# A two-layer decoder trunk: the last residual product of each layer as seven block products of sums

## The chip, the cores and the metric

The kernel runs on one core of one Trainium2 chip. The metric is the time of one launch in microseconds of device time. A measurement of this kernel is the median of a few runs.

## The reference

All data is fp32; 512 tokens, a width of 1024, two layers.

```python
# per layer
x = x + (g_conv*y_conv + g_attn*y_nsa + g_mla*y_mla) @ w_out      # "the mix"
x = x + memory_cross_attention(rmsnorm(x), rmsnorm(mem), ...)     # ends with @ w_xo
gate, up = split(rmsnorm(x, norm_ffn) @ w_gate_up, 2)             # 1024 -> 2 x 2816
x = x + (silu(gate) * up) @ w_down                                # 2816 -> 1024, "the down residual"
# after two layers
return rmsnorm(x, norm_final)
```

The change is about the last line of a layer, the product of the 512x2816 activation with `w_down`, added to `x`.

## The kernel before

**Products.** Every fp32 operand is split in two (`hilo`): a high part, cast by ACT (line 92), and the rest, subtracted by DVE (line 93). A product of two operands is three matmuls, high x high, high x low and low x high (lines 85 to 87 in `mm3`, 1143 to 1145 in `residual`). Weights come by a DMA on SP's queue into `raw` (`load`, two buffers of 1 MB) and are split there into `wh` and `wl` (`unit`, three buffers each, 128x1024).

**The down residual** (`residual`, line 1125). `row_units` loads two blocks of 128 rows of `w_down` at a time, all 1024 columns, 4 KB a row. For each of the 22 row blocks PE runs over four token tiles and two halves of columns; the eight sums fill all eight PSUM banks. The last two or three blocks are held back and run tile by tile, so that the tiles end one after another; after each, DVE adds the bank to `x` (line 1157) and `after(t)` stores the tile in layer 0, and normalises and stores it in layer 1. The activations were split in the FFN stage (`keep_act`), block by block, into slots that other tiles had left.

**Sums in DRAM.** The gate/up product is already made in seven block products. The sums of the blocks of `w_gate_up` that it needs lie in DRAM (`sums`) and are made by DMAs on POOL's queue, DRAM to DRAM, half of them plain copies and half accumulating: 128 DMAs of 320 KB a layer. They are paced: every product of three matmuls calls `tick`, and every fifth (from layer 0's down residual on every sixth) issues the next DMA, which waits for that matmul. In the stages of the FFN none is issued.

**Order.** A scheduler orders each engine's instructions ahead of time; an engine runs its queue strictly in that order. SP carries the loads of weights, POOL the paced DMAs, the stores of `x` between stages (`xd`) and the power of -1/2 of each norm (line 200, `rs`).

## Time and profile before

| | |
|---|---|
| median of 3 runs | 1941.39 us (1939.9 to 1941.57) |
| the profiled execution | 1943.2 us, of which the span 1941.5 us |
| PE, PE weight loads | 1913.9 us (99%), 1674.5 us (86%) |
| DVE, ACT, POOL | 71%, 50%, 12% |
| granted TensorE clock | 0.996 of full speed |
| DMA | 317.95 MB, mean 164 GB/s |
| chain that ended last | PE 80%, DVE 8%, issue 5%, DMA 4%, ACT 3% |

The span is from the first to the last instruction of the profiled execution. PE is the engine of the matmuls, PEld its weight loads, which overlap matmuls; DVE, ACT and POOL are the vector, scalar and GpSimd engines, SP issues DMAs. A layer's stages follow one another: the mix (to about 545 us in layer 0), cross attention, the FFN's gate/up (about 632 to 855), the down residual (855.1 to 975.9), then layer 1 with its down residual from 1812 to the end.

### The profile page before, as it was taken

How to read it: one execution, taken by the hardware profiler on the slowest of the kernel's cores; microseconds unless marked ns; L12 is line 12 of the kernel's file. 1: busy time of each engine (PE TensorE's matmuls, PEld its weight loads, DVE VectorE, ACT ScalarE, POOL GpSimd, SP SyncE). 2: the span in 40 equal slices, each digit the busy share in tenths (PEclk: the TensorE clock that was granted, in tenths of full speed). 3: DMA queues.
4: the chain of work that ended last, by engine and by line, in shares of the span. 5: the costliest groups of instructions: out<-in, count | busy, mean ns of one | idle time of the engine just before them, and what ended most of it. 6: DMA issues, size and time to landing. Idle time of an engine off the chain costs nothing.

```text
span 1941.5 us, 29100 instructions
## 1 busy us (share of the span) xinstructions
PE 1913.9 (99%) x11136; PEld 1674.5 (86%) x11136; DVE 1371.0 (71%) x2525; ACT 979.2 (50%) x1858; POOL 227.6 (12%) x380
## 2 busy tenths in 40 slices
PE   9999999999999999999999999999999999999998
PEld 8877888888887999998888878888888889999886
DVE  6989899764466877762279989986655677777523
ACT  5366557663355545541244755675634465545312
POOL 1211112112121000001211111111112010000000
PEclk9999999999999999999999999999999999999999
DMA  6676655567783455566666565445676525555531
GB/s 186 152 188 182 154 134 137 132 169 211 221 229 113 154 175 192 177 226 176 175 168 162 161 189 127 122 102 141 170 204 181 177 99 173 179 182 174 183 108 65
DMA packets 218871, 317.95 MB, mean 164 GB/s; under 512 B 14528, under 2 KB 172483, under 8 KB 218732
## 3 DMA queue, kind: packets, MB, share of 16 engines
q1 hardware_dynamic: 194028, 220.83, 34.8%
q0 software_dynamic: 21760, 88.10, 21.0%
q10 hardware_dynamic: 2944, 7.17, 1.1%
q8 instruction: 87, 1.43, 0.3%
q14 instruction: 52, 0.43, 0.1%
HBM read 307.64 MB, written 92.30 MB: 206 GB/s over the span
## 4 chain that ended last, share of the span: by engine, by line
PE 80%; DVE 8%; issue 5%; DMA 4%; ACT 3%; POOL 1%; SPq 0%; DVEq 0%; POOLq 0%; ACTq 0%
PE ps_mm L85 12%; PE ps_mm L87 12%; PE ps_mm L86 12%; PE ps_mm L1143 2%; PE ps_mm L1144 2%; PE ps_mm L1145 2%; PE ps_t L85 2%; PE ps_t L86 2%; PE ps_t L87 2%; PE ps_s L85 2%; PE ps_s L86 2%; PE ps_s L87 2%; DMA raw<-in_w_in_dram 2%; PE ps_t L960 2%; PE ps_t L1144 2%
## 5 line engine op out<-in xcount | busy, mean ns | idle before, releaser
L93 DVE TENSOR_TENSOR wl<-raw,wh 128x1024 fp32r<-128x1024 f32 (+5 forms) x382 | 451.2, 1185 | 377.2 <-ACT wh L92 375.7
L92 ACT CAST wh<-raw 128x1024 fp32r<-128x1024 f32 (+5 forms) x382 | 388.0, 1020 | 587.5 <-PE ps_pv L1145 198.7
L85 PE MATMUL ps_mm<-hTh,wh 128*128 128x512 f32 (+1 forms) x1152 | 415.4, 361 | 1.1 <-DVE kc L93 1.1
L87 PE MATMUL ps_mm<-hTh,wl 128*128 128x512 f32 (+1 forms) x1152 | 411.4, 358 | 0.8 <-DVE wl L93 0.8
L86 PE MATMUL ps_mm<-hTl,wh 128*128 128x512 f32 (+1 forms) x1152 | 412.0, 358 | 0.0
L87 PEld LDWEIGHTS ps_mm<-hTh,wl 128*128 128x128 f32 x1152 | 218.2, 190 | 33.4 <-DVE wl L93 1.9
L85 PEld LDWEIGHTS ps_mm<-hTh,wh 128*128 128x128 f32 x1152 | 218.5, 190 | 30.4 <-DVE kc L93 1.5
L86 PEld LDWEIGHTS ps_mm<-hTl,wh 128*128 128x128 f32 x1152 | 218.5, 190 | 26.5 <-issue 0.7
L356 POOL DMA_DIRECT2D sums<-in_w_gate_up_dram x192 | 119.6, 627 | 842.1 <-PE ps_mm L87 429.6
L463 DVE SCALAR_TENSOR_TENSOR ca<-u,vT,ca 128x512 f32<-128x512 f32 x240 | 177.1, 745 | 2.9
L923 ACT ACTIVATE P<-P,ss 128x512 f32<-128x512 f32 (+3 forms) x128 | 71.4, 558 | 55.9 <-DVE ss L920 55.0
L92 ACT CAST PTh<-ps_t 128x512 fp32r<-128x512 f32 (+4 forms) x136 | 70.4, 517 | 55.8 <-PE ps_t L960 45.0
L85 PE MATMUL ps_s<-rh,wh 128*128 128x256 f32 x320 | 90.6, 283 | 0.0
L86 PE MATMUL ps_s<-rl,wh 128*128 128x256 f32 x320 | 90.6, 283 | 0.0
L87 PE MATMUL ps_s<-rh,wl 128*128 128x256 f32 x320 | 90.6, 283 | 0.0
L356 POOL DMA_DIRECT2D sums<-sums x64 | 50.0, 782 | 275.4 <-PE ps_mm L87 130.1
L93 DVE TENSOR_TENSOR PTl<-ps_t,PTh 128x512 fp32r<-128x512 f32 (+2 forms) x120 | 71.3, 596 | 8.4 <-ACT PTh L92 7.5
L931 ACT ACTIVATE P<-P,sr 128x512 f32<-128x512 f32 (+3 forms) x128 | 63.1, 553 | 18.2 <-DVE sr L929 18.1
L85 PE MATMUL ps_mm<-op,wh 128*128 128x512 f32 (+1 forms) x192 | 68.7, 358 | 0.0
L86 PE MATMUL ps_mm<-op,wh 128*128 128x512 f32 (+1 forms) x192 | 68.2, 355 | 0.0
L87 PE MATMUL ps_mm<-op,wl 128*128 128x512 f32 (+1 forms) x192 | 68.1, 355 | 0.0
L200 POOL TENSOR_TENSOR rs<-rs,mhalf 128x1 f32<-128x1 f32 x32 | 23.1, 721 | 383.5 <-DVE rs L197 383.3
(553 smaller groups left out, 4574.1 us busy)
## 6 DMA issues: line engine op xcount, KB each, us to landing
sums<-in_w_gate_up_dram POOLq DMA_DIRECT2D x192, 320.0 KB, 4.4
raw<-sums SPq DMA_DIRECT2D x80, 512.0 KB
raw<-in_w_in_dram SPq DMA_DIRECT2D x32, 1024.0 KB
raw<-in_w_gate_up_dram SPq DMA_DIRECT2D x24, 1024.0 KB
raw<-in_w_down_dram SPq DMA_DIRECT2D x22, 1024.0 KB
sums<-sums POOLq DMA_DIRECT2D x64, 320.0 KB, 4.9
raw<-in_w_in_dram SPq DMA_DIRECT2D x26, 512.0 KB
raw<-in_w_gate_up_dram SPq DMA_DIRECT2D x20, 512.0 KB
```

What stands on the lines that cost most here:

```text
L85: nc.tensor.matmul(o, lh, rh, start=start, stop=False)
L86: nc.tensor.matmul(o, lh, rl, start=False, stop=False)
L87: tick(nc.tensor.matmul(o, ll, rh, start=False, stop=stop))
L92: nc.scalar.copy(hi, src)
L93: nc.vector.tensor_tensor(lo, src, f(hi), op=OP.subtract)
L356: d = nc.gpsimd.dma_start(dst, src, accum_op=op) if op else nc.gpsimd.dma_start(dst, src)
L463: nc.vector.scalar_tensor_tensor(c, u[:, j:j + T], cw[:, m, j:j + 1], c, op0=OP.mult, op1=OP.add)
L923: nc.scalar.activation(p[:, c], p[:, c], AF.Exp, bias=s[:, k:k + 1], scale=-1.0, accum_out=s[:, 4 + k:5 + k])
L931: nc.scalar.activation(P[k], P[k], AF.Copy, scale=r[:, k:k + 1])
L960: nc.tensor.transpose(tp[:, w:w + 128], P[k][:, j * 128:(j + 1) * 128], ident)
L1143: nc.tensor.matmul(o, xh, wh[:, r], start=k == 0, stop=False)
L1144: nc.tensor.matmul(o, xh, wl[:, r], start=False, stop=False)
```

## The change

The down residual becomes a 2x2 block product: the 22 row blocks of `w_down` are taken as even and odd ones, its columns as two halves, the tokens as two halves of 256. Seven products of sums take the place of eight. Four of the seven need sums of quarters of `w_down`: four more tensors in DRAM (`down`, 128-row blocks of 512 columns at a pitch of 528), made by the same paced DMAs, 88 a layer of 256 KB, after the 128 for gate/up. The activation's sides are made in the FFN stage by `keep_act` (two split, the others as plain sums) and, for products 2 to 6, split in the residual during the product before. The products run one behind the other, 11 row blocks by two token tiles each, in two PSUM banks at a time; the results are added to `x` (and to a partial sum `U`) behind each product. Weights come in quarters: per product three loads of 1, 1 and 0.75 MB with rows of 2 KB. The pace is every 4th product instead of the 5th, every 12th in the FFN stage (where before nothing was issued), and every 4th instead of the 6th from layer 0's down residual on.

```diff
+        W, V = w_gate_up[l], w_down[l]
+        up = [dr.tile([512, n], F32, name=f"up{l}_{i}") for i in range(4)]
+        down = [dr.tile([FFN // 2, 528], F32, name=f"down{l}_{i}")[:, 0:512] for i in range(4)]
+        def added(s, w):
+            for dst, src in ((s[0], w[1][0]), (s[2], w[0][0]), (s[1], w[0][0]), (s[3], w[0][1])):
+                yield dst, src, None
+            for dst, src in ((s[0], w[1][1]), (s[2], w[1][0]), (s[1], s[0]), (s[3], s[1])):
+                yield dst, src, OP.add
...
+            for j in range(FFN // 256):
+                yield from added([t[j * 128:(j + 1) * 128, :] for t in down],
+                                 [[V[(2 * j + e) * 128:(2 * j + e + 1) * 128, o:o + 512] for e in range(2)]
+                                  for o in (0, 512)])
...
+    def down_residual(W, sums, kept, xs, more_x, after):
...
+        def split(v):
+            h, lo = (new("op", (128, 2, 256), F32R, name=n)[:, 0:v.shape[1], :] for n in ("th", "tl"))
+            hilo(h, lo, v)
+            return h, lo
+        def fourth(n):
+            v = new("P", (128, 2, 256), name="t2")[:, 0:b11[n].shape[1], :]
+            nc.vector.scalar_tensor_tensor(v, b11[n], -1.0, b22[n], op0=OP.mult, op1=OP.subtract)
+            return split(v)
+        parts = [(quarters[0][:, :, low[0]], lambda n: None), (quarters[1][:, :, low[0]], fourth), (of[1], lambda n: split(b12[n])),
+                 (of[2], lambda n: split(b21[n])), (quarters[1][:, :, low[1]], lambda n: split(b11[n])),
+                 (of[0], lambda n: split(b22[n])), (of[3], lambda n: None)]
+        tags = (("t", "t"), ("s", "s"), ("mm", "mm"), ("mm", "pv"), ("t", "t"), ("s", "s"), ("mm", "mm"))
...
+        def done(i, t, p):
+            x, y = xs[t], xs[2 + t]
+            if i == 0:
+                U[t] = new("op", name="U")
+                nc.scalar.copy(U[t], p)
+                add(x[0], x[0], p)
+            elif i == 1:
+                add(x[0], x[0], p)
+            elif i == 2:
+                add(U[t], U[t], p)
+                later(y[0], U[t])
+            elif i == 3:
+                add(U[t], U[t], p)
+                later(x[1], U[t], OP.subtract)
+                later(y[1], U[t], OP.subtract)
+            elif i == 4:
+                add(x[1], x[1], p, OP.subtract)
+                after(t)
+            elif i == 5:
+                add(y[0], y[0], p)
+                add(y[1], y[1], p, OP.subtract)
+            else:
+                add(y[0], y[0], p)
+                after(2 + t)
...
+            for n in range(N):
+                j = 2 * n
+                if n % 2 == 0:
+                    m = min(4, nj - j)
+                    raw = load(lambda raw: [(raw.rearrange("p (k c) -> p k c", k=4)[:, 0:m], w[:, j:j + m, :])])
+                m = min(2, nj - j)
+                c = n % 2 * 1024
+                held.append((n, unit(raw[:, c:c + m * 512].rearrange("p (k c) -> p k c", k=m), (m, 512))))
+                then.append(ahead(n))
...
+    EVERY = 4
-    paced["every"] = 5
+    paced["every"] = EVERY
...
+        paced["every"] = 12
...
+        def keep_act(m, a, b, sign=1.0):
+            d = act_slot(m)
+            for i in range(2):
+                q = slice(i * 256, (i + 1) * 256)
+                nc.vector.scalar_tensor_tensor(d[i], a[:, q], sign, b[:, q], op0=OP.mult, op1=OP.mult)
+            hilo(d[2], d[3], d[0])
+            if m % 4 == 3 or m == FFN // 128 - 1:
+                (b11, b12), (b21, b22) = (h[0:2] for h in kept[-1])
+                tc.cur_priority += 100000
+                nc.vector.tensor_tensor(b11, b11, b12, op=OP.subtract)
+                nc.vector.tensor_tensor(b21, b22, b21, op=OP.subtract)
+                nc.vector.tensor_tensor(b21, b21, b11, op=OP.add)
+                nc.vector.tensor_tensor(b12, b22, b12, op=OP.subtract)
+                tc.cur_priority -= 100000
...
-            paced["every"] = 6
+            paced["issued"], paced["every"] = 0, EVERY
...
-        residual(lambda k: act[k], FFN // 128, w_down[l], xs, after, 3 if last else 2, {8: lambda: load_x(xd, xs)})
+        down_residual(w_down[l], down_sums, kept, xs, lambda: load_x(xd, xs), after)
```

DVE's queue in the down residual of layer 1, before: the end of the FFN stage, the 19 subtractions that are left (`wl`), and the first additions to `x`.

```order
L93 TENSOR_TENSOR a_18550<-k,a_18550 128x512
L93 TENSOR_TENSOR a_18568<-k,a_18568 128x512
L93 TENSOR_TENSOR wl<-raw,wh 128x1024 x19
L1157 TENSOR_TENSOR x<-x,ps_t 128x512 x2
L197 SCALAR_TENSOR_TENSOR rs<-ss 128x1
L213 SCALAR_TENSOR_TENSOR hn<-x,rs,gB 128x512 x2
```

And after, around the end of the fourth product (index 3); `tl` is the low part of an activation sum for the next product.

```order
L1212 TENSOR_TENSOR U<-U,ps_mm 128x512
L1212 TENSOR_TENSOR U<-U,ps_pv 128x512
L93 TENSOR_TENSOR wl<-raw,wh 128x1024 x2
L93 TENSOR_TENSOR tl<-a_18028,th 128x512
L93 TENSOR_TENSOR wl<-raw,wh 128x1024
L93 TENSOR_TENSOR tl<-a_19010,th 128x256
L1212 TENSOR_TENSOR x<-x,U 128x512
L93 TENSOR_TENSOR tl<-a,th 128x512
L1212 TENSOR_TENSOR x<-x,U 128x512
L93 TENSOR_TENSOR tl<-a,th 128x512
L93 TENSOR_TENSOR wl<-raw,wh 128x1024
```

Around the end of the sixth product (index 5) four additions stand in one row:

```order
L93 TENSOR_TENSOR wl<-raw,wh 128x1024
L93 TENSOR_TENSOR wl<-raw,wh 128x512
L93 TENSOR_TENSOR wl<-raw,wh 128x1024
L1212 TENSOR_TENSOR x<-x,ps_s 128x512 x4
L93 TENSOR_TENSOR wl<-raw,wh 128x1024 x4
```

Before, nothing stood between the weights' subtractions; now the splits of the activations and the additions stand between them.

POOL's queue around the cross-attention residual of layer 0, before: the last two sums, the stores of `x`, the four `rs` of the FFN's norm.

```order
L356 DMA sums_1_148<-sums_0_147 64x1280
L356 DMA sums_3_150<-sums_1_148 64x1280
L1298 DMA xd<-x 128x512 x3
L200 TENSOR_TENSOR rs<-rs,mhalf 128x1
L1298 DMA xd<-x 128x512
L200 TENSOR_TENSOR rs<-rs,mhalf 128x1
L1298 DMA xd<-x 128x512 x3
L200 TENSOR_TENSOR rs<-rs,mhalf 128x1
```

And after, with the new sums between them:

```order
L1416 DMA xd<-x 128x512 x2
L368 DMA down_0_151<-in_w_down_dram 128x512
L200 TENSOR_TENSOR rs<-rs,mhalf 128x1
L1416 DMA xd<-x 128x512 x2
L368 DMA down_2_153<-in_w_down_dram 128x512
L200 TENSOR_TENSOR rs<-rs,mhalf 128x1
L1416 DMA xd<-x 128x512
L368 DMA down_1_152<-down_0_151 128x512
L1416 DMA xd<-x 128x512 x2
L200 TENSOR_TENSOR rs<-rs,mhalf 128x1
```

The `rs` operations now stand behind DMAs that wait for a matmul, and one of them for the landing of another sum.

## Rows read from the trace of the kernel before

**Rows 1.** The page: span; busy us, share of the span and instructions of PE

```profile
span 1941.5 us, 29100 instructions
PE 1913.9 (99%) x11136; PEld 1674.5 (86%) x11136; DVE 1371.0 (71%) x2525; ACT 979.2 (50%) x1858; POOL 227.6 (12%) x380
```

**Rows 2.** Busy time by stage: down residuals of layers 0 and 1, FFN

```profile
core 0: us, PE busy (x) PEld busy (x) DVE busy (x) ACT busy (x) POOL busy (x), PEclk, DMA share, GB/s
855.10:975.90 120.80, 120.15 (x531) 99.08 (x530) 37.20 (x40) 28.20 (x36) 21.18 (x38) 1.00 0.67 187
1811.90:1931.80 119.90, 119.54 (x530) 98.50 (x530) 37.54 (x41) 28.67 (x38) 1.11 (x3) 1.00 0.28 100
640.00:860.00 220.00, 219.35 (x1812) 218.36 (x1811) 167.85 (x207) 111.67 (x163) 0.00 (x0) 1.00 0.56 181
```

**Rows 3.** Timeline of PE in layer 1's down residual: start, us, engine, line

```profile
1854.84 0.39 PE L1145 MATMUL ps_mm<-wh,al 128*128 128x512 f32 x1
1855.07 0.39 PE L1143 MATMUL ps_mm<-wh,ah 128*128 128x512 f32 x1
```

**Rows 4.** Waits of ACT and DVE, 858 to 966: us in total, times, longest

```profile
ACT wh L92 <- PE ps_pv L1145: 83.8, 20, 4.5
...
DVE wl L93 <- ACT wh L92: 76.5, 19, 4.3
```

**Rows 5.** Groups by line and shape, whole span: busy us, mean ns of one

```profile
L93 DVE TENSOR_TENSOR wl<-raw,wh 128x1024 fp32r<-128x1024 f32 x354 | 431.8, 1223 | 374.0 <-ACT wh L92 372.5
L92 ACT CAST wh<-raw 128x1024 fp32r<-128x1024 f32 x354 | 370.4, 1050 | 547.9 <-PE ps_pv L1145 194.3 <-PE ps_mm L86 99.8 <-DMA raw<-in_w_gate_up_dram 43.3
...
L1423 DVE TENSOR_TENSOR k<-ps_s,k 128x256 f32<-128x256 f32 x40 | 17.0, 424 | 1.4
L93 DVE TENSOR_TENSOR al<-k,ah 128x512 fp32r<-128x512 f32 x26 | 16.8, 684 | 0.0
...
L92 ACT CAST ah<-k 128x512 fp32r<-128x512 f32 x26 | 15.9, 620 | 0.1
...
L1157 DVE TENSOR_TENSOR x<-x,ps_mm 128x512 f32<-128x512 f32 x18 | 12.0, 678 | 0.0
```

**Rows 6.** DMA queues and issues, 855 to 960: packets, MB, share of 16 engines

```profile
q0 software_dynamic: 1925, 7.89, 36.3%
q1 hardware_dynamic: 4668, 11.30, 30.4%
...
sums<-in_w_gate_up_dram POOLq DMA_DIRECT2D x19, 320.0 KB, 4.2
sums<-sums POOLq DMA_DIRECT2D x6, 320.0 KB, 4.6
```

**Rows 7.** The same view, 884 to 888, where one accumulating DMA runs alone

```profile
q0 software_dynamic: 89, 0.37, 56.7%
```

**Rows 8.** Timeline around one gate/up load of 1 MB

```profile
785.50 0.37 SPq L101 DMA_DIRECT2D raw<-in_w_gate_up_dram  x1
...
790.64 1.05 ACT L92 CAST wh<-raw 128x1024 fp32r<-128x1024 f32 x1 [3.19 <-DMA raw<-in_w_gate_up_dram]
...
791.73 2.44 DVE L93 TENSOR_TENSOR wl<-raw,wh 128x1024 fp32r<-128x1024 f32 x2
...
794.61 0.28 PE L85 MATMUL ps_mm<-hTh,wh 128*128 128x256 f32 x1
```

**Rows 9.** Busy time of 20 us in layer 0's mix, columns as in rows 2

```profile
540.00:560.00 20.00, 20.00 (x134) 18.39 (x134) 11.20 (x18) 7.46 (x15) 5.12 (x7) 1.00 0.95 268
```

**Rows 10.** DMA issues in the FFN stage, 700 to 850

```profile
raw<-in_w_gate_up_dram SPq DMA_DIRECT2D x7, 1024.0 KB
```

**Rows 11.** Timeline of the end: the last matmul and the last addition

```profile
1933.40 0.39 PE L1145 MATMUL ps_pv<-wh,a 128*128 128x512 f32 x1
...
1934.30 0.68 DVE L1157 TENSOR_TENSOR x<-x,ps_pv 128x512 f32<-128x512 f32 x1
```

**Rows 12.** Timeline of POOL behind layer 0's cross-attention residual

```profile
628.26 0.54 POOL L1298 DMA_DIRECT2D xd<-x  x1 [2.09 <-DVE rs L197]
628.82 0.57 POOL L200 TENSOR_TENSOR rs<-rs,mhalf 128x1 f32<-128x1 f32 x1
```

More of the change, by code (lines that the diff above doesn't have):

```diff
@@ L355, in tick @@
             for dst, src, op in islice(paced["steps"], 1):
+                paced["issued"] += 1
                 d = nc.gpsimd.dma_start(dst, src, accum_op=op) if op else nc.gpsimd.dma_start(dst, src)
@@ L1173 @@
     xs = load_x(xin, [], (0,))
-    sums, paced["steps"] = summed(0)
-    paced["every"] = 5
+    sums, down_sums, paced["steps"] = summed(0)
+    paced["every"] = EVERY
     for l in range(L):
@@ L1302 @@
         last = l == L - 1
[L1303 removed]
+        assert paced["issued"] >= 128
+        paced["every"] = 12
         g_next = load_gain(norm_final if last else norm_mix[l + 1])
[L1305 to L1331 removed]
@@ new lines, with act_slot @@
+        kept = []
+        def act_slot(m):
+            if m % 4 == 0:
+                kinds = [(plain, F32)] * 2 + [(halved, F32R)] * 2
+                if m + 4 <= FFN // 128:
+                    group = [[home(*kind) for kind in kinds] for _ in range(2)]
+                else:
+                    group = [[t[:, i:i + 1, :] for t in (home(*kind) for kind in kinds[::2]) for i in range(2)]
+                             for _ in range(2)]
+                kept.append(group)
+            return [v[:, m % 4 // 2, :] for v in kept[-1][m % 2]]
@@ L1432 @@
                 nc.scalar.activation(g[j][:, q1], g[j][:, q1], AF.Silu)
-                nc.vector.scalar_tensor_tensor(g[j], g[j], -1.0, ka[j], op0=OP.mult, op1=OP.mult)
-                keep_act(m + j, g[j])
-        xs = []
+                keep_act(m + j, g[j], ka[j], -1.0)
+        assert not list(paced["steps"])
         if not last:
-            sums, paced["steps"] = summed(1)
-            paced["every"] = 6
-        if not last:
+            sums, next_down, paced["steps"] = summed(1)
+            paced["issued"], paced["every"] = 0, EVERY
             def after(t):
@@ L1448, in after @@
                     nc.sync.dma_start(out[0, t * 128:(t + 1) * 128, c * 512:(c + 1) * 512], h)
[L1449 removed]
+        xs = []
+        down_residual(w_down[l], down_sums, kept, xs, lambda: load_x(xd, xs), after)
+        if not last:
+            down_sums = next_down
         x_src = xd
```

109 lines of the change are left out of this document (66 added, 43 removed).

## The prediction

> **What bounds the kernel now.** I read first the page's busy shares [rows 1], then the busy time by stage [rows 2], the matmuls' rhythm [rows 3], what ACT and DVE wait for inside the stage that is changed [rows 4], the price list of the small operations [rows 5], and last the DMA queues of each stage [rows 6, 7, 9, 10], with two short pieces of the timeline at the places that the change makes thinner [rows 8, 12]. PE is busy 1913.9 us of a span of 1941.5, at a granted clock of 1.00 in every stage that I use, the upper of its two levels. In both down residuals PE is busy 120.15 of 120.80 us and 119.54 of 119.90 [rows 2]: there is no idle time to win there, only matmuls to leave out. ACT and DVE are at a quarter to a third of that stage, and both wait backwards, for PE: the cast into `wh` waited 83.8 us, 20 times, for a matmul to give a buffer back, and the subtraction into `wl` only follows the cast [rows 4]. So before, weights are early by 4 us per unit; that is the cover that the change spends.
>
> **Removed: 132 matmuls.** Before, a layer's residual has 22 x 4 x 2 x 3 = 528 products of 128x512; after, 7 x 11 x 2 x 3 = 462. Layer 0's stage lasts 120.80 us, so 0.2288 us each (the starts of two neighbours stand 0.23 apart [rows 3]; the 0.39 us of a record overlaps the next and is not the price). 66 x 0.2288 = 15.1 us a layer, **-30.2 us** for two. Nothing else lies beside these matmuls, so all of it is on the path as long as PE stays fed.
>
> **Tail.** Before, two additions of 0.68 us follow the last matmul, which starts at 1933.40, and the span ends 8.1 us later [rows 11]. After, the last product ends a token tile with one addition per half, tiles 0 and 1 long done: one addition less behind the end, about **-0.5 us**.
>
> **Added work on DVE and ACT in the residual.** A product of 66 matmuls takes 15.1 us. In that time DVE has five units of 1.223 and a half one of 0.68 (6.8 us), for most products the split of the activations for the next product (5.5 x 0.684 = 3.8), once a fourth sum (5.5 operations of the same size, 3.8), and 2 to 6 additions of 0.678 (1.4 to 4.1) [rows 5]. Seven products: 47.6 + 19.2 + 3.8 + 22 x 0.68 = 85.6 us of 105.7; the fullest, product 2 of 7, has 6.8 + 3.8 + 3.8 + 1.4 = 15.8 of 15.1. ACT has 5.5 x 1.05 + 5.5 x 0.62 = 9.2 of 15.1. So on the mean it fits, but DVE's spare time per unit falls from 4.0 us (76.5 in 19 [rows 4]) to (105.7 - 85.6) / 38.5 = 0.5. What is queued matters: behind product 6 of 7 four additions (2.7 us) stand in one row ahead of the next four `wl`; PE has 12 matmuls (2.7 us) per unit and up to three units in buffers. The lower bound is 0 (buffers cover it), the upper one 0.7 for the overfull product and 0.7 for each other of six boundaries: 5 us a layer. The trace has no such row; nearest are the waits of [rows 4], with 4 us of cover, so I take a little: 1.5 a layer, **+3**.
>
> **Added DMA traffic in layer 0's residual.** There the paced sums for the next layer run beside the weights. Before, the software queue took 36.3% of 105 us for 25 paced DMAs, 1.52 us of all engines each, and the hardware queue 30.4% for 11.30 MB, 2.82 us per MB [rows 6]. After, each weight byte range is read as seven half-width blocks: 7 x 2.75 MB (MiB) = 20.2 MB instead of 11.5, so 57 us; and 154 of the counted products fall here, every fourth issues one: 38 x 1.52 = 58 us. Sum 115 us for a stage of 105.7 us. That is over full, by 9 us if no paced DMA slips into the next stage, and less if some do (nothing waits for them there until much later). Against a large loss: the mix of before ran a slice of 20 us at a DMA share of 0.95 with PE busy 20.00 [rows 9]. Bounds 0 and 9; I take **+6**, nearer the upper, since the loads have only two buffers. In layer 1's residual nothing is paced, 57 of 105.7 us: nothing added.
>
> The Trainium skill, "DMA: Bandwidth & Descriptors", section "Queues, rings and completion order", says that each DMA engine goes round its queues packet by packet. If so, the sums' larger packets win: in [rows 6] a software packet took 16 x 38.1 / 1925 = 0.32 us and a hardware one 16 x 31.9 / 4668 = 0.11, so that a load that meets a backlog would get a quarter of the engines, the loads and not the sums would be late, and the term would be its upper 9 and not 6.
>
> **Added DMA traffic in the FFN stage.** 40 of a layer's 88 new sums (256 KB each, 1.52 x 0.8 = 1.2 us of the engines) are issued there, one per 12 products, 36 matmuls of 0.121 us [rows 2] or 4.4 us. The stage's DMA share goes from 0.56 by 40 x 1.2 / 220 to about 0.78. Its thin place is the 1 MB load of `w_gate_up`: issued 785.50, cast at 790.64 after a wait of 3.19 for it, its `wl` ready at 792.95 (half of the pair that starts at 791.73), and PE takes it at 794.61: 1.7 us of slack [rows 8]. Seven such loads fall in 150 us [rows 10], ten in a stage. One paced DMA beside it costs 1.2 us, mostly hidden; an accumulating one by [rows 7] 0.567 x 4.0 = 2.3, times 0.8 is 1.8, just over. Bounds 0 and, with every load 0.6 late from two of them, 6 a layer; I take 1 a layer, **+2**.
>
> **Moved: POOL's queue at the cross-attention residual.** The new sums run on past the point where the old ones had ended, so the four `rs` operations of the FFN's norm stand in POOL's row behind paced DMAs that wait for a matmul and, when accumulating, for a landing 4.2 to 4.6 us after issue [rows 6]. Before, only stores stood there, and the third `rs` ran at 628.82, right after one [rows 12]; behind it queue DVE's normalisation and PE's transposes. A dependent sum comes one or two steps (2.7 or 5.5 us) behind its source, so some stand in front for up to 2 us and most for none. Bounds 0 and 5 a layer; 0.5 each, **+1**. **The mix** paces every fourth product and not every fifth, and 48 new sums end there: [rows 9] shows that it is already full in places and PE fed; bounds 0 and 6, **+1**. **In the FFN** `keep_act` has, per block of 128 rows, operations of 1.94 us in place of 1.36 (by their sizes, at 0.68 for 128x512 and 0.42 for half of it [rows 5]): 22 x 0.58 = 13 us a layer on a DVE that was busy 168 of 220 us [rows 2]. The 52 idle hide it, so nothing; without that cover it would be 13.
>
> **The sum.** 1943.2 (the profiled execution) - 30.2 - 0.5 + 3 + 6 + 2 + 1 + 1 = 1925.5 us. The median of before is 1941.39, 1.8 below that execution: **1923.7 us**.
>
> **Rivals.**
> *A, clean.* The covers hold, 2 us lost in all: 1941.4 - 30.7 + 2 = 1912.7. For it: [rows 9], a full DMA slice without a PE gap, and three unit buffers. Against it: 115 us of transfers in 105.7.
> *B, DVE or the loads fall behind steadily.* The products' boundaries cost their bound (10 for both layers), layer 0's residual 9 to 10, and FFN loads 4: 23 lost, 1934. For it: the 15.8 us of DVE work in 15.1. Against it: the mean of 85.6 in 105.7.
> *C, slower: the DMA engines cannot carry layer 0's residual.* An accumulating sum takes 2.27 us of all engines by itself [rows 7]. If under load every paced DMA costs that, 38 x 2.27 = 86, with the weights' 57 it is 143 us, 37 over the 105.7; with 3 + 2 of the others, 1941.4 - 30.7 + 42 = 1953. It decides from a loss of 31 us in all, that is a paced DMA of about 2.0 us in the mean. Against it: half the sums are plain copies, and the mean of 25 was 1.52.
> Beside this stands what the same page's "Specifications" give, about 358 GB/s of HBM traffic for a core. By it, with a plain sum counted as read and written and an accumulating one as read twice and written, the stage would move 20.2 + 38 x 0.82 = 51 MB, an estimate of 143 us, as in C. The trace speaks against it as a limit on the sum of both directions: the accumulate of [rows 7] moved 0.37 MB in 2.27 us, three passes of it, 490 GB/s.
> *D, no difference*: some 25 to 30 us lost from several of these, 1937 to 1942.
>
> **How the numbers follow.** Forecast (1917 to 1929) 0.52, A 0.20, B (1929 to 1937.5) 0.17, D 0.04, C 0.07. Differences under 0.2% (3.9 us) cannot be told from none by a measurement of this kernel, so faster means below 1937.5: 0.52 + 0.20 + 0.17 = 0.89; the same 0.04; slower 0.07. The range reaches from A's lower side, 1911, to 1935, which leaves out C, D and the upper end of B.
>
> **What would show it.** PE's records fall by 132; the two residuals last 105 to 108 us (layer 1) and 108 to 117 (layer 0), the difference being the paced traffic. In layer 0's residual the DMA share is 0.95 or more, and `wh` there waits for `raw`, where in layer 1 it waits for PE. At the start of products 2 to 6 PE's weight loads wait for `wl` or `tl` on DVE. In the FFN stage some of PE's first matmuls of an iteration wait for `wl`, by under 2 us. The prediction is wrong if layer 1's residual lasts over 112 us (the DVE row is mis-sized), if layer 0's is as short as layer 1's (contention mis-sized), or if the FFN stage grows by over 5 us a layer.

## The result: 1.1% slower

The changed kernel takes **1963.19 us** in the median (1961.27 to 1966.47, four runs) where the kernel before takes 1941.48 beside it: a ratio of **1.0114, interval 1.0102 to 1.0126**. The forecast was 1923.7, with a range from 1911 to 1935. The profiled execution took 1961.27 us, its span is 1959.5 us. One execution of the experiment e6 took 5255.62 us and is left out of its figures.

The page of after; the lines answer to [rows 1], with the two DMA queues below (packets, MB, share of 16 engines) and the chain that ended last:

```profile
span 1959.5 us, 29631 instructions
PE 1897.5 (97%) x11004; PEld 1649.7 (84%) x11004; DVE 1479.3 (75%) x2757; ACT 1035.7 (53%) x1962; POOL 348.0 (18%) x556
...
q1 hardware_dynamic: 208428, 238.13, 37.1%
q0 software_dynamic: 41472, 134.25, 32.3%
...
PE 68%; DMA 13%; DVE 10%; ACT 4%; issue 3%; POOL 1%; SPq 0%; POOLq 0%; DVEq 0%; ACTq 0%
```

The 132 matmuls are gone (11136 to 11004), but PE's busy time fell by 16.4 us and not by 30, and the chain that ended last has 13% DMA in place of 4%: PE now waits for transfers. Busy time of layer 0's residual, layer 1's residual and layer 0's FFN stage, the rows that answer to [rows 2]:

```profile
core 0: us, PE busy (x) PEld busy (x) DVE busy (x) ACT busy (x) POOL busy (x), PEclk, DMA share, GB/s
868.50:990.65 122.15, 110.66 (x467) 85.75 (x465) 85.56 (x117) 59.28 (x88) 27.66 (x47) 1.00 0.94 284
1843.10:1949.40 106.30, 105.89 (x464) 86.13 (x462) 85.05 (x118) 59.13 (x88) 3.48 (x3) 1.00 0.59 191
641.50:868.50 227.00, 222.43 (x1831) 221.19 (x1830) 173.95 (x250) 108.34 (x167) 26.66 (x39) 0.99 0.77 221
```

Layer 1's residual is what the arithmetic promised: 106.3 us, PE fed, DMA share 0.59. Layer 0's has the same instructions, takes 122.15, and PE is busy for only 110.66 of it. All stages, from the starts of PE's matmuls at their borders (us, in the profiled executions; the cross attention includes the product with `w_out` before it):

| | mix 0 | cross 0 | FFN 0 | residual 0 | mix 1 | cross 1 | FFN 1 | residual 1 | tail |
|---|---|---|---|---|---|---|---|---|---|
| before | 489.0 | 146.6 | 219.5 | 120.8 | 474.8 | 142.2 | 220.1 | 120.7 | 7.9 |
| after | 491.5 | 150.0 | 227.0 | 122.2 | 483.0 | 150.0 | 219.5 | 106.3 | 10.1 |
| after - before | +2.5 | +3.4 | +7.5 | +1.4 | +8.2 | +7.8 | -0.6 | -14.4 | +2.2 |

The sum is +18.0 us. Layer 1's residual got 14.4 us shorter, of the 15.1 that each should have gained; layer 0's got 1.4 longer, 16.5 behind that. Every stage in which sums of `w_down` are made, or sums are paced more densely, is longer (mix 0's 2.5 and cross 0's 3.4 lie within the scatter between profiles, told below); layer 1's FFN, with one paced DMA, is not.

What ACT and PE wait for in layer 0's residual (868 to 991), the rows that answer to [rows 4]:

```profile
ACT wh L92 <- DMA raw<-down: 26.9, 10, 5.9
ACT wh L92 <- DMA raw<-in_w_down_dram: 14.4, 6, 4.6
...
PE ps_mm L1256 <- DVE wl L93: 4.6, 6, 0.8
PE ps_mm L1255 <- ACT wh L92: 2.9, 3, 1.8
```

Before, the casts waited for PE to give a buffer back; now they wait for loads, 41.3 us in 16, and PE waits for the casts and subtractions. The DMA queues of 868 to 973, against [rows 6]:

```profile
q1 hardware_dynamic: 9322, 18.35, 50.5%
q0 software_dynamic: 2480, 10.16, 39.2%
...
up<-in_w_gate_up_dram POOLq DMA_DIRECT2D x25, 320.0 KB, 6.2
...
up<-up POOLq DMA_DIRECT2D x8, 320.0 KB, 5.1
```

### The profile page after: what moved, and what is told of

The parts are those of the page before. It is cut to its first block, busy times and chain, and to the rows that moved or that the text cites. A ratio compares the mean times of both kernels' runs of the same rounds, so it can differ in the third digit from the quotient of the medians.

```text
span 1959.5 us, 29631 instructions
## 1 busy us (share of the span) xinstructions
PE 1897.5 (97%) x11004; PEld 1649.7 (84%) x11004; DVE 1479.3 (75%) x2757; ACT 1035.7 (53%) x1962; POOL 348.0 (18%) x556
## 4 chain that ended last, share of the span: by engine, by line
PE 68%; DMA 13%; DVE 10%; ACT 4%; issue 3%; POOL 1%; SPq 0%; POOLq 0%; DVEq 0%; ACTq 0%
PE ps_mm L87 12%; PE ps_mm L85 12%; PE ps_mm L86 12%; DVE wl L93 4%; DMA raw<-in_w_in_dram 3%; DMA raw<-down 2%; ACT wh L92 2%; PE ps_s L85 2%; PE ps_s L86 2%; PE ps_s L87 2%; PE ps_t L86 2%; PE ps_t L87 2%; PE ps_t L85 2%; PE ps_t L972 2%; DMA raw<-in_w_down_dram 2%
## 5 line engine op out<-in xcount | busy, mean ns | idle before, releaser
L93 DVE TENSOR_TENSOR wl<-raw,wh 128x1024 fp32r<-128x1024 f32 (+3 forms) x422 | 490.6, 1169 | 285.5 <-ACT wh L92 284.1
L92 ACT CAST wh<-raw 128x1024 fp32r<-128x1024 f32 (+3 forms) x422 | 422.1, 1008 | 536.6 <-PE ps_mm L86 117.2
L368 POOL DMA_DIRECT2D up<-in_w_gate_up_dram x192 | 120.0, 628 | 483.5 <-PE ps_mm L87 342.7
L368 POOL DMA_DIRECT2D down<-in_w_down_dram x132 | 89.9, 742 | 241.9 <-PE ps_mm L87 91.9
L368 POOL DMA_DIRECT2D up<-up x64 | 49.7, 776 | 260.0 <-PE ps_mm L87 127.4
L93 DVE TENSOR_TENSOR PTl<-ps_t,PTh 128x512 fp32r<-128x512 f32 (+2 forms) x120 | 71.3, 596 | 12.2 <-ACT PTh L92 11.1
L85 PE MATMUL ps_mm<-op,wh 128*128 128x512 f32 (+1 forms) x192 | 68.7, 358 | 0.0
L368 POOL DMA_DIRECT2D down<-down x44 | 36.1, 821 | 182.4 <-DMA down<-down 52.2
```

Source lines behind the costliest of these rows:

```text
L85: nc.tensor.matmul(o, lh, rh, start=start, stop=False)
L92: nc.scalar.copy(hi, src)
L93: nc.vector.tensor_tensor(lo, src, f(hi), op=OP.subtract)
L368: d = nc.gpsimd.dma_start(dst, src, accum_op=op) if op else nc.gpsimd.dma_start(dst, src)
```

## The experiments

Theory T, as the prediction had it: the time of the 16 DMA engines; where paced sums and loads together need more than the engines give, PE stalls. Rival P: POOL's queue, where norms stand behind sums that wait for a landing. Rival S: the new loads and the split work are slow by themselves. Theory L came up on the way. "Unpaced" is short for the kernel of e3. Stages are from one profile each. Stages with the same code and the same sums differed by up to 6 us between profiles (mix 0: 491.5 in after, 497.8 in e2; cross 1: 143.7 in e7, 149.9 in e11), and the time of one kernel by up to 15 us between executions, so only differences above that, or repeated ones, are read.

### e1 and e2: no sums of w_down, sparse and dense pace

```diff
-            for j in range(FFN // 256):
-                yield from added([t[j * 128:(j + 1) * 128, :] for t in down], ...)
...
-    (of[1], ...), (of[2], ...), ..., (of[0], ...), (of[3], ...)
+    (quarters[0][:, :, low[1]], ...), (quarters[0][:, :, low[0]], ...), ..., (quarters[1][:, :, low[0]], ...), (quarters[0][:, :, low[1]], ...)
-    EVERY = 4          # e1 only; every 6th from layer 0's residual on. e2 keeps 4
+    EVERY = 5
```

> The changed kernel with the sums of w_down left out: none of the 88 DMAs a layer is issued, and the four products that took them load quarters of w_down of the same size and form instead (so those products are of other blocks). The pace of the gate/up sums is that of the kernel before (every 5th product, every 6th from layer 0's residual on). Theory T (the engine time of the DMAs: paced sums and weight loads together are more than the 16 engines give, loads come late and PE stalls): layer 1's residual stays at 106 us, layer 0's falls from 122.2 to about 108 to 112 (25 paced DMAs instead of 38), the FFN stage of layer 0 from 227.0 to 219.5, the mixes and cross attentions back to their times of before; in all 1941.5 - 14.4 - 10 + 2 = about 1918 us. Rival P (the norms' small operations on POOL stand behind sums that wait for a landing): layer 0's residual stays near 122, only the ends of the mixes and the cross attentions get shorter, about 1948. Rival S (the new loads in pieces of 2 KB and the split work on DVE are slow by themselves): near 1960.

> The kernel without sums of w_down (quarters of w_down are loaded in their place, 1925.5 us), but with the denser pace of the change, every 4th product in the mixes and in layer 0's residual. Only the pace differs. If the pace in the residual counts, DMA for DMA: 38 in place of 25 there, the stage grows from 114.5 to about 119 to 122; mixes and cross attentions, which hold the same 128 sums in a shorter time, +0 to 3 us each: 1931 to 1938. If the sums of w_down themselves do it (their loads from DRAM sums, their size, their place in the order), the stage stays near 115 and the time near 1926.

e1: 1925.51 us, ratio 0.9921 (0.9905 to 0.9937). FFN 0 is 219.5, cross attentions 146.7 and 142.9, mixes 488.7 and 475.2, all as before: S falls, and so does P for the residual. But layer 0's residual is 114.5, where T said 108 to 112, with the 25 paced DMAs that cost the old one nothing (1.7 us of it is a fall of the clock). The row of 858 to 972:

```profile
858.00:972.00 114.00, 108.30 (x464) 86.48 (x463) 85.72 (x118) 60.44 (x92) 20.40 (x35) 0.99 0.89 267
```

e2: 1949.23 us, ratio 1.0042 (1.0026 to 1.0059). The pace alone costs 24 us, 11 more than the most that was expected: residual 0 goes to 128.7 (3.4 of it falls of the clock), mix 0 to 497.8, mix 1 to 482.4; the FFN stages stay at 219.5 and the cross attentions at 145.5 and 143.3, where no sums of `w_down` are made. So the residual's loss does not need the sums of `w_down`, and the FFN's and the cross attentions' does.

### e3: nothing paced in layer 0's residual

```diff
-            paced["issued"], paced["every"] = 0, EVERY
+            paced["issued"], paced["every"] = 0, 10 ** 6
...
             down_sums = next_down
+            paced["every"] = EVERY
```

> The changed kernel, complete, but no paced DMA is issued during layer 0's down residual; layer 1's 216 sums are issued every 4th product in its mix and cross attention and every 12th in its FFN stage, as in layer 0. Theory T: layer 0's residual falls from 122.2 to 106 or 107 us, the same as layer 1's, and layer 1's FFN stage grows from 219.5 to about 227, since 40 sums now fall there: about 1961 - 16 + 7 = 1952. Rival P: layer 0's residual stays over 115, since what is queued there on DVE and ACT is unchanged; about 1960. Rival S: the same as P.

1937.82 us, ratio 0.9985 (0.9973 to 0.9998): the stage does what T said, and the whole gains more than expected. Residual 0 takes 105.0 us, as layer 1's; FFN 1 takes 226.6, since its 40 sums fall there now; and mix 1, with the same pace of 4, is back at 475.2. This last repeats: the five kernels here that pace nothing in layer 0's residual (e3, e7, e8, e11, e13) have a mix 1 of 475.1 to 476.8, while the six that pace 38 sums there, half of them accumulating (after, e2, e4, e10, e14, e15), have 477.0 to 483.0. So the denser pace alone does not make the 8.2 us of after. The rows of the stage (872.0 to 977.1) and its casts' waits:

```profile
872.00:977.10 105.10, 105.10 (x467) 86.86 (x466) 85.21 (x117) 60.04 (x88) 3.11 (x9) 1.00 0.66 214
```

```profile
ACT wh L92 <- DMA raw<-down: 9.5, 6, 3.5
ACT wh L92 <- PE ps_mm L1257: 7.5, 4, 4.2
```

DVE's 85.21 us and ACT's 60.04 are all there, and PE is busy for the whole stage: rival S is out. The paced DMAs take the whole 16 us of layer 0's residual.

### e4: all sums out before the FFN stage

```diff
-    EVERY = 4
+    EVERY = 3          # layer 0's mix and cross attention; 4 from its residual on
```

> The changed kernel, complete, with every 3rd product paced instead of every 4th in the mixes and cross attentions of layer 0 (in layer 0's residual every 4th, as before, and in layer 1's mix every 4th), so that all 216 sums of layer 0 are out before its FFN stage. Theory T: the FFN stage of layer 0 falls from 227.0 to 219.5 us; mix and cross attention of layer 0, where the sums' rate goes up by a third, grow by 2 to 10 us; in all 1957 to 1966. Rival P: the ends of the mix and the cross attention of layer 0, where the norms stand behind sums, grow by some us each, and the FFN stage falls too (it has no norm): 1958 to 1964. The two differ in where mix 0 grows: T at weight loads (casts that wait for a load), P at the norms.

1985.90 us, ratio 1.0233 (1.0212 to 1.0254). FFN 0 is 219.5 as expected, so its 7.5 us are the sums in it. But mix 0 takes 511.4 and cross 0 161.9, 20 and 12 more than after, far over what either theory gave. In the mix the casts wait longer for loads, as T said (22.5 us for `w_in` between 60 and 510; after 12.1), at a mean DMA share of only 0.74. In cross 0 it is rival P: PE waits 13.0 us at once for a norm that stands behind sums on POOL. The row of mix 0, and PE's longest wait of 511 to 673:

```profile
0.00:490.00 490.00, 468.10 (x2388) 392.07 (x2389) 384.18 (x868) 276.09 (x580) 118.08 (x201) 0.98 0.74 191
```

```profile
PE ps_t L221 <- DVE hn L213: 13.6, 2, 13.0
```

### e5: copies in place of accumulations

```diff
-                yield dst, src, OP.add
+                yield dst, src, None
```

> The changed kernel with every accumulating DMA turned into a plain copy of the same size at the same place (so the sums are not sums, and the output is of other products); count, pace and waits unchanged. Theory T, with the accumulating half as the costly one: the software queue's share falls from 32.3% to about 24%, layer 0's residual from 122 to about 112 us, its FFN stage from 227 to 223, layer 1's mix from 483 to 478; in all about 1942. Theory T with bytes as the cost (a copy hinders loads as much as an accumulation): times as with the change, 1958 to 1964. Rival P: the landing waits on POOL stay (each copy still reads what another writes), so nothing but noise, 1958 to 1964, with the stops of POOL still in the trace.

1925.76 us, ratio 0.9920 (0.9896 to 0.9944), q0 at 22.3%. Outside the residual the mixes (487.0 and 472.2) and the cross attentions (143.3 and 143.2) lie between 3.4 us below before and 1 above, and FFN 0 keeps 4 us (223.6). So the accumulating half makes most of the loss there. Whether by the engines' time or by the norms behind it this run does not part: POOL still waits for landings, but PE's wait for `hn`, the normalised tiles, in cross 1 is 0.7 us, where after has 4.6. The residual, with 38 copies, does not move: 122.1. (One fall of the clock lies in it, 0.97 over the stage, 3 to 4 us; after has none there.) Its row, 860 to 982:

```profile
860.00:982.00 122.00, 111.31 (x470) 86.56 (x469) 84.95 (x117) 60.29 (x93) 22.30 (x48) 0.97 0.86 284
```

A share of 0.86 is not full, and the stage is as long as at 0.94, or 118 to 119 without the fall of the clock, where T said 112. T fails in the residual.

### e12 (and e9): the old residual in layer 0 under the same load

```diff
-        down_residual(w_down[l], down_sums, kept, xs, lambda: load_x(xd, xs), after)
+        if last: down_residual(w_down[l], both[1][1], kept, xs, lambda: load_x(xd, xs), after)
+        else: residual(lambda k: act[k], FFN // 128, w_down[l], xs, after, 3 if last else 2, {8: lambda: load_x(xd, xs)})
...
+    both = [summed(0), summed(1)]
+    paced["steps"] = chain(islice(both[0][2], 128), both[1][2])     # no w_down sums in layer 0
```

The pace in layer 0's old residual is every 3rd product in e9, every 4th in e12; e12 also takes four blocks of sums in turn (e6) and halves those in FFN 1.

> A complete kernel with the old down residual in layer 0 (whose loads take half the engines' time of the new one) and the new one in layer 1 only, so that sums of w_down are made for one layer. The paced DMAs run from layer 0's mix at every 5th product, then 12 of layer 1's; none in layer 0's FFN stage; every 3rd product in layer 0's old residual (58 DMAs), every 5th in layer 1's mix and cross attention, the last 6 or so in layer 1's FFN stage at every 12th. Theory T: layer 1's residual 106 (-14.4), tail +2, layer 0 as before up to its residual, that residual still 121 to 123 since its loads have 11 us for each MB, layer 1's mix and cross attention +3 to 6, FFN +1: 1931 to 1937. Rival P: the cross attention of layer 1 loses 8 us as with the change, mix 8: 1942.

> The kernel with the new residual in layer 1 only (1951.5 us; its longest stall was 12.5 us at the layer boundary, a norm's small operation on POOL behind backlogged sums), now with the steps of four blocks in turn, every 4th product in layer 0's old residual in place of every 3rd, and the 20 steps that are left for layer 1's FFN stage in halves at every 6th. Rival P (POOL's queue): the stall at the boundary goes, with the drop of the clock behind it: 1941.5 - 14.4 + 2 + 3 = about 1932. Theory T alone (the old residual at this rate is full, so that loads are late): little changes, 1945 or more.

e9: 1951.54 us, ratio 1.0046 (1.0029 to 1.0063), with a stall of 12.5 us at the layer boundary, where a norm waits; both theories gave less. e12: 1947.75, ratio 1.0029 (1.0019 to 1.0039); that stall is gone, as P said, but another of 7.3 us came in cross attention 0. The total is T's (1945 or more), though not for T's reason, since the residual loses nothing. Both hold the comparison that settles the residual: the old form with 44 (e9) and 38 (e12) paced DMAs in 105 us. Busy time (e9, 855 to 975.8; e12, 867.6 to 988.4), the waits of its casts (the same line in both but for the line number), and e12's DMA issues:

```profile
855.00:975.80 120.80, 120.30 (x530) 98.92 (x528) 35.08 (x39) 28.98 (x39) 35.58 (x56) 1.00 0.88 246
867.60:988.40 120.80, 120.04 (x528) 99.05 (x528) 37.43 (x40) 27.72 (x34) 31.36 (x53) 1.00 0.84 221
```

```profile
ACT wh L92 <- PE ps_pv L1164: 83.8, 20, 4.5
```

```profile
q0 software_dynamic: 2966, 12.16, 53.0%
...
up<-in_w_gate_up_dram POOLq DMA_DIRECT2D x30, 320.0 KB, 3.9
raw<-in_w_down_dram SPq DMA_DIRECT2D x9, 1024.0 KB
up<-up POOLq DMA_DIRECT2D x8, 320.0 KB, 6.4
```

120.80 us and 83.8 us of waiting for PE, to the digit what [rows 2, 4] show with 25. At a share of 0.84 and of 0.88 the old form loses nothing; at 0.89 the new one loses 9 (e1). **Theory L**: not the engines' time is short but the time of one load. The old form uses a load of 1 MB in 11 us, the new one in 5.5, and there are two raw buffers. From the trace's packets, a 1 MB load of layer 0's new residual takes from its issue to its last packet 4.7 us in the mean when nothing is paced (e3, 105.0 us), 6.3 with 25 paced (e1, 114.5), 6.5 with 38 copies (e5, 122.1 with a fall of the clock), 7.2 with 38 half of which accumulate (after, 122.2; e2, 128.7). In e9 a load of the old form takes just as long, 7 us in the mean and 10.5 at most, and costs nothing, because PE needs the next one only after 11.

The issues on SP's queue show the loop of the two buffers. In after a buffer comes round every 12.2 us in the mean: 7 for the load, and 5.1 (4.5 at the least) until its casts and subtractions let SP issue the next load into it. In e3, where PE is fed, it comes round every 10.8. In e9's old form the same 7 us stand in a round of 21.2.

Cross attention 0 of e12 shows what a row of accumulations does to a load, one of `w_xq` that SP issued at 541.54. Timeline of ACT and of POOL:

```profile
558.14 1.04 ACT L92 CAST wh<-raw 128x1024 fp32r<-128x1024 f32 x1 [11.97 <-DMA raw<-in_w_xq_dram]
```

```profile
545.36 0.82 POOL L375 DMA_DIRECT2D up<-in_w_gate_up_dram  x1 [0.56 <-PE ps_mm L87]
547.58 0.77 POOL L375 DMA_DIRECT2D up<-in_w_gate_up_dram  x1 [1.41 <-PE ps_mm L87]
549.80 0.78 POOL L375 DMA_DIRECT2D up<-in_w_gate_up_dram  x1 [1.45 <-PE ps_mm L87]
551.60 0.77 POOL L375 DMA_DIRECT2D up<-in_w_gate_up_dram  x1 [1.02 <-PE ps_mm L87]
```

Products follow each other faster there, so the pace by count gives an accumulation every 2 us, and the load of 1 MB lands only as the last of them does. The completions of its 16 DMA engines stand in the trace: ten had landed by 552.1, the last two at 557.9 and 558.1. So a load waits for the slowest engine, which a mean share of 16 does not show. The accumulations, after the first, were late too, 6.5 to 8.2 us from issue to landing, where the copies just before them took 3.1.

### e6 and e7: no stops for landings on POOL

```diff
-                yield from added(...)                      # block by block
+            for i in range(0, 16, 4):
+                yield from chain(*zip(*blocks[i:i + 4]))   # four blocks in turn
```

> The changed kernel, complete, with the steps of four blocks of sums taken in turn, so that an accumulating DMA stands four or more steps behind the one that it needs and POOL's queue does not stop for a landing; bytes, pace and all else unchanged. Theory T: layer 0's residual and FFN stage unchanged (122 and 227 us), only single waits behind POOL go (3.4 us at the end of layer 1's mix): 1956 to 1962. Rival P: POOL's stops are the larger part of the loss, mixes and cross attentions return to their times of before, and layer 0's residual, where the sums no longer bunch, too: under 1950.

> The kernel with layer 0's residual unpaced (its time was 1937.8 us), and in addition the steps of four blocks of sums taken in turn, so that POOL's queue hardly stops for a landing; the same bytes. Theory T: stages as with the unpaced kernel within 2 us each, only single waits behind POOL go: 1934 to 1939. Rival P: POOL's stops cause the losses of 4 to 8 us in each cross attention and 4 in layer 0's mix; these go, 1922 to 1928.

e6, on the changed kernel: 1968.02 us in the median of three (1955.71 to 1968.45), ratio 1.0115 (1.0080 to 1.0151), no better than the change; its stages are not known. e7, on the unpaced kernel: 1939.06 us, ratio 0.9978 (0.9960 to 0.9996), the same as e3 and at the upper edge of what T said. Cross 1 falls from 150.1 to 143.7, as P said, but FFN 0 grows from 228.4 to 233.8: four blocks in turn put sixteen accumulations in one row. POOL's stops are not the bulk of the change's loss, but of cross 1's 7.8 us in after they are the larger part: a `hn` behind mix 1's product with `w_out` waits 3.63 us for a POOL that waited 4.74 for a landing. POOL in after, then PE's wait for `hn` in cross 1 in after and in e7 (before has none there):

```profile
1514.37 0.81 POOL L368 DMA_DIRECT2D down<-down  x1 [4.74 <-DMA down<-down]
1514.90 1.37 POOL L368 DMA_DIRECT2D down<-in_w_down_dram  x2
1516.00 0.86 POOL L200 TENSOR_TENSOR rs<-rs,mhalf 128x1 f32<-128x1 f32 x1
```

```profile
PE ps_t L221 <- DVE hn L213: 4.6, 2, 3.4
```

```profile
PE ps_t L221 <- DVE hn L213: 0.7, 2, 0.5
```

It is not the only way to lose time there: in e3's cross 1, of 150.1 us, PE waits 0.8 us for `hn`, but 2.5 for a late subtraction, 1.8 for a late cast, and the clock falls.

### e8 and e11: the sums of w_down in halves

```diff
-            for j in range(FFN // 256):
+            for j, r in pairs(range(FFN // 256), (0, 64)):      # e8: all of them, twice the pace
...
+                    paced["halves"] += [(dst[r:r + 64, :], src[r:r + 64, :], op) for r in (0, 64)]   # e11: in the FFN stages only
```

Both stand on the unpaced kernel; e11 also has four blocks in turn.

> The kernel with layer 0's residual unpaced (1937.8 us), and in addition the sums of w_down made in halves: twice as many DMAs of 128 KB, paced twice as densely (every 2nd product, every 6th in the FFN stage), the same bytes in the same time. If a load is late because one whole DMA of 256 KB runs beside it (theory T with bursts), the FFN stages fall from 227 to about 222 and the cross attentions by 2 us each, about 1925 to 1930. If only the mean share of the engines matters (theory T with the mean), nothing changes, 1936 to 1940. If each DMA costs POOL and the engines a fixed part, it gets slower, 1940 to 1950.

> The kernel with layer 0's residual unpaced and the steps of four blocks of sums taken in turn (1939 us; FFN stages 233.8 and 222.2 in its profile), with the sums that fall in the FFN stages made in halves of 128 KB at twice the rate, as in the kernel with halves everywhere, whose FFN stages took 220.5 and 222.5. If a burst of one DMA is what makes the FFN's thin load late: FFN stages 220 to 223 each, 1922 to 1932. If the halves' gain there came from something else (sums already out by then): 1936 to 1942.

e8: 1986.16 us, ratio 1.0224 (1.0198 to 1.0250). The FFN stages fall to 220.5 and 222.5, and the cross attentions rise to 170.9 and 175.5: twice as many DMAs, half of which wait for a landing, back POOL up until the norms behind them stop PE for 16.4 us in one piece. This is rival P at work (640 to 870; in the whole span PE waits 47.8 us for `hn`), and it is far outside what was expected of any theory:

```profile
PE ps_t L221 <- DVE hn L213: 17.0, 2, 16.4
```

e11: **1935.05 us, ratio 0.9955 (0.9937 to 0.9973)**, the fastest complete kernel here, but between the two forecasts. FFN 1 is 220.7, as expected of smaller pieces, FFN 0 227.6, which is not.

### e13 and e14: copies and accumulations in turn

```diff
+            for b in blocks:
+                b = list(b)
+                for i in range(4):
+                    yield b[i]
+                    if behind: yield behind[i]
+                behind = b[4:]
+            yield from behind
```

e13 is the unpaced kernel with halves in the FFN stages and this order; e14 the changed kernel with this order alone.

> The kernel with layer 0's residual unpaced and halves in the FFN stages (1935 us with four blocks in turn), now with the steps in an order in which a copy of one block alternates with an accumulation of the block before it: no two accumulating DMAs in a row, and each stands two or more steps behind what it needs. If bunches of accumulations make loads late (theory B): cross attentions 144 to 147 us, FFN stages 220 to 222, 1924 to 1930. If only the number counts (theory T): within 3 us of 1935.

> The changed kernel, complete, with only the order of the steps changed, as in the alternating kernel; pace and sizes are those of the change, layer 0's residual paced too. Theory L with the pace (each paced DMA beside the thin loads costs about 0.4 us): layer 0's residual stays at 118 to 124 us; the mixes and cross attentions fall, in all 1948 to 1956. Theory B: the residual falls too, to 110 to 114, in all 1938 to 1945.

e13: 1936.78 us, ratio 0.9983 (0.9970 to 0.9996). The FFN stages are 222.8 and 220.3; the cross attentions stay at 149.2 and 150.9, though no two accumulations follow each other. Of cross 1's loss 5.5 us are again PE's wait for `hn` (4.0 at once), this time behind a sum that waits for a matmul; POOL, 1578 to 1581:

```profile
1578.46 0.81 POOL L380 DMA_DIRECT2D down<-down  x1 [6.83 <-PE ps_mm L1169]
```

The total is T's, the FFN stages are close to B's. e14: 1962.90 us, ratio 1.0112 (1.0097 to 1.0126), residual 0 at 123.0, as theory L said; the whole is the change's, which neither theory said. In the residual the order does nothing; the number does (e1, e2). In the cross attentions no order takes the loss away for certain: in e7, e13 and e14 cross 1 has 143.7, 150.9 and 145.9. The FFN rows of e13, against 0.77 of the engines and 227.0 us in after:

```profile
643.20:866.00 222.80, 221.19 (x1830) 219.84 (x1829) 173.72 (x250) 108.75 (x167) 54.30 (x80) 1.00 0.79 227
1602.70:1823.00 220.30, 219.92 (x1812) 218.76 (x1811) 174.46 (x252) 109.58 (x166) 53.29 (x79) 1.00 0.79 230
```

The same bytes, the same share, and 4 to 7 us less: the share does not set the loss. That the size of what a load meets at once does is the likely reason; e11's FFN 0, with the same halves, speaks against it as the only one.

### e10 and e15: weight loads in two DMAs

```diff
-   load(lambda raw: [(raw.rearrange(...)[:, 0:m], w[:, j:j + m, :])])
+   load(lambda raw: [(raw.rearrange(...)[:, a:min(a + 2, m)], w[:, j + a:j + min(a + 2, m), :]) for a in range(0, m, 2)])
```

> The changed kernel, complete, with each weight load of the new residual issued as two DMAs of half the rows, so that the first half can be cast while the second is under way; bytes, pace and all else unchanged. Theory L (the loss in layer 0's residual is one of latency: with two raw buffers a load may take only so long from its issue to its cast, and every paced DMA beside it makes it longer; the engines need not be full): the first cast of a load comes about 1 us earlier, the stage falls from 122.2 to 115 to 119 us; 1957 to 1961. Theory T (the engines are full): the stage stays at 121 to 123, since the bytes are the same; 1961 to 1966.

> The kernel with split weight loads again, for a second profile (1948.7 to 1963.8 in eight executions before, the profiled one the slowest). Theory L: in an execution near the median of 1953 the residual of layer 0 lasts 115 to 118 us, and the other stages are those of the change. Otherwise the residual stays at 121 to 123 and the difference lies in the mixes and cross attentions, where nothing was changed, so that it would be the scatter between executions.

e10: 1953.06 us, ratio 1.0064 (1.0045 to 1.0083), 10 us under the change. Its profiled execution (1963.77) was its slowest, with residual 0 at 121.7; in e15 (1954.01) it was 118.7. That is the direction of theory L, but 3.5 us of the 10, and both stages are longer than was expected; the rest lies in mix 1 (482.1 and 477.3), right behind the residual, and in scatter. It supports L weakly and settles nothing by itself. A third raw buffer, which would be the direct proof, was not tried.

## Why the prediction was wrong

**Removed matmuls: right.** 132 fewer; where nothing is paced a residual takes 105.0 to 106.3 us (105.7 by the forecast).

**DVE and ACT work in the residual (+3): too much.** PE waited 0.3 us for DVE in layer 1's residual, and e3 fed PE for 105.10 of 105.10 us. The cover of 0.5 us a unit was enough.

**DMA traffic in layer 0's residual (+6, bounds 0 and 9): the step that failed.** It measured 16.5 us in after and 17 against e3. The loads' price was right (18.35 MB took 50.5% of 105 us, 2.89 us per MB), a paced DMA's too high: 33 took 39.2%, 1.25 us each and not 1.52. At these prices the prediction's own sum is 106 us for a stage of 105.7, a loss of nothing. So what failed was the rule that the stage loses only what goes beyond the engines' whole time. The old form loses nothing at 0.84 and 0.88 (e12, e9), the new one 9 at 0.89 (e1) and 17 to 24 at 0.86 to 0.94 (e5, after, e2; without falls of the clock 13 to 20). The limit is the time of a load: two raw buffers and 5.5 us a load, where the old form had 11. The prediction had the halved time in its hands (57 us of loads in 105.7 in place of 32 in 121) and used it only as a share.

The Trainium skill's rule that each DMA engine goes round its queues packet by packet ("DMA: Bandwidth & Descriptors", section "Queues, rings and completion order") was taken for its upper bound of 9, with the loads late and the sums not. The trace agrees by half: a 1 MB load went from 4.7 to 7.2 us, but a plain sum, too, from 4.2 [rows 6] to 6.2 us from issue to landing. The loss was about twice the bound.

Two readings beside it were off. [Rows 7] do not hold one accumulating DMA alone but the end of one and most of the next, 0.37 MB where one is 0.33, so that one costs about 2.0 us of the engines and not 2.27. And the 490 GB/s beside rival C divide by the engines' time; by the clock, three passes of 0.37 MB in 4 us are 278. What does speak against the limit weighed there is after itself: 18.35 MB of loads and 10.16 MB of sums, half of them copies, are some 44 MB read and written in 105 us, an estimate of 417 GB/s.

**FFN (+2): mis-sized, and once counted wrong.** Layer 0 lost 7.5 us. Layer 1 lost none: its sums, begun in the residual, were out before. The mechanism was the expected one, the thin load of 1 MB. Timeline of after, ACT then PE, against [rows 8]:

```profile
722.04 1.99 ACT L92 CAST wh<-raw 128x1024 fp32r<-128x1024 f32 x2 [6.66 <-DMA raw<-in_w_gate_up_dram]
```

```profile
721.02 0.28 PE L87 MATMUL ps_pv<-rh,wl 128*128 128x256 f32 x1
723.14 0.38 PE L85 MATMUL ps_mm<-hTh,wh 128*128 128x256 f32 x1 [1.83 <-ACT wh L92]
...
724.40 0.58 PE L87 MATMUL ps_mm<-hTh,wl 128*128 128x256 f32 x1 [0.76 <-DVE wl L93]
```

The sum allowed 0.6 us for a late load; one late load here cost 2.6 us of stall, and then the clock fell.

**Mixes and cross attentions (+2, bounds 0 to 16 for both layers): measured +21.9.** One slice at a share of 0.95 with PE fed [rows 9] was taken as proof that the mix bears it. The slice, from 540, is not even in the mix, whose last matmul starts at 537.3, and 20 us show only that nothing waited in them. e2, without sums of `w_down`, loses 8.8 and 7.6 in the mixes against before. In mix 1 after loses 8.2; PE waits there for weights (3.1 us at once at 1122, 1.6 at 1063), and the clock falls behind each. In POOL's term, priced 0.5 a layer for the FFN's norm, the mechanism was right but the place was not: in layer 1 PE waits 4.6 us for `hn`, near the bound of 5, and 3.4 of them at the norm behind the mix; layer 0 has 0.7 in place of the 3.2 of before.

**Tail (-0.5): +2.2.** The normalisation of the tile before, behind which the last addition stands as it did before, now begins with the last matmul (1949.2) and not 1.0 us ahead of it, so that this addition begins 1.25 us after that matmul's start where it was 0.9; timeline of DVE:

```profile
1949.12 1.42 DVE L213 SCALAR_TENSOR_TENSOR hn<-x,rs,gB 128x512 f32<-128x512 f32 x2 [0.67 <-POOL rs L200]
...
1950.45 0.68 DVE L1212 TENSOR_TENSOR x<-x,ps_mm 128x512 f32<-128x512 f32 x1
```

Up to the last normalisation that makes about 1 us. e1 ends with the same instructions and has a tail of 8.3; what makes 1.8 us behind the last DVE instruction in after stays open.

**The rivals.** C had the right sign, the wrong mechanism and the wrong spread: 17 us and not 37 in the residual, at 1.25 us a paced DMA and not 2.27, the rest in six other places, each priced near nothing. That its 1953 came nearest to 1963 is luck. D's price, "some 25 to 30 us lost", was passed as well: 48 us lost between the two profiles. The chance of slower (0.07) was too small because every bound was drawn for its stage alone, with PE's present calm as the argument, and that calm rested on slack which this change used up in six places at once.

**Settled and open.** Shown: the residual's loss is the paced DMAs beside loads with half the old time (e3, e9, e12), by their number (e1, e2) and not their order (e14), and at most 4 of its 17 us by their kind (e5). Shown: outside it the accumulating half is the greater part of the cost (e5, which also takes away what the accumulations of before had cost; 4 us stay in FFN 0), and in the FFN smaller pieces mostly cost less (e8, e13, and one of two stages in e11). Argued from the traces, without a run of its own: two buffers as the exact reason in the residual. Open: why cross 1 loses 7 us and more in most profiles, through POOL in some and through late loads in others; why mix 1's loss comes with the pacing of the residual ahead of it; and why the tail has 8.2 us in some kernels and 10 in others with the same end.

## What to carry over

A transfer moved into "idle" DMA time is priced by the slack of the loads that it meets, not by the share of the engines: at a share of 0.88 to 0.89 one form lost nothing (e9) and the other 9 us (e1). List, per stage, the time between a load's issue and its need, with the number of buffers, and compare it with the load's time as it is beside the traffic (here 7 us, 4.7 alone). An edit that halves the work per loaded byte halves that slack. Pace background transfers in small pieces where loads are thin and leave them out where they are thinnest: here that, with the sums of four blocks in turn, turned a loss of 1.1% into a gain of 0.45% (e11). And look at what stands behind them on the queue that issues them.

## What the runs showed of the hardware

A stall of PE can be paid twice: behind the one of 2.6 us at 721 us in after the granted clock falls, 0.91 in the mean over the slice, and the same behind one of 3.1 us at 1122:

```profile
720.00:740.00 20.00, 17.41 (x131) 17.00 (x131) 15.52 (x22) 9.74 (x15) 1.90 (x3) 0.91 0.70 210
1120.00:1140.00 20.00, 16.58 (x75) 13.42 (x75) 17.01 (x33) 15.40 (x31) 2.57 (x6) 0.91 0.44 114
```

0.09 of 20 us is 1.8 us beside the stall, lost while the lower of the two levels (1.2 GHz) is granted. Not every stall has this behind it: after the one of 3.4 us at 1514 to 1518 the clock stays at 1.00. A load of 1 MB takes 4.7 us alone in e3's residual; in e12 a cast waited 12 us for one beside accumulating DMAs in a row, and the slowest of 16 engines ended it. And the time of a kernel with thin loads scatters: e11's ten runs lie between 1924.1 and 1939.1, where the kernel before keeps within 1939 and 1946.
